# A decoder trunk on one core: the order of the first loads and of the first work on ScalarE, and the number of idle transposes

## The chip, the cores and the metric

The kernel runs on one core of a Trainium2 chip. The metric is the device time of one execution in microseconds (us); less is better. The engines are named as the profile names them: PE (TensorE, with PEld for its weight loads), DVE (VectorE), ACT (ScalarE), POOL (GpSimd) and SP (SyncE, which here issues nearly all DMAs of the opening; SPq is its queue).

## The reference

Two layers of a decoder on 256 tokens of width 2048, all in float32. Cut to what matters here:

```python
def rms_norm(x, g):
    y = x * lax.rsqrt(jnp.mean(x * x, axis=-1, keepdims=True) + EPS)
    return y * g

def hybrid_layer(x, attn_norm, w_in, ..., w_o, mlp_norm, w_up, w_down):
    h = rms_norm(x, attn_norm)
    proj = h @ w_in                      # 2048 -> 6160 columns, split in eight parts
    ...                                  # gated linear attention and stick-breaking attention
    x = x + mixed @ w_o
    hm = rms_norm(x, mlp_norm)
    return x + jnp.square(jax.nn.relu(hm @ w_up)) @ w_down

def reference(x, ...):                   # x: (1, 256, 2048)
    for l in range(2):
        x = hybrid_layer(x, ...)
    return x
```

## The kernel before

**The products.** Every float32 operand is split in a high part, rounded to the type that PE takes in one pass, and a low part, the rest. A product of a weight block with x is then three matmuls into the same accumulator: x high with weight high (L577), x high with weight low (L578), x low with weight high (L579). ACT makes high parts, DVE makes low parts. For the weights this is done in `weight_parts`: L558 is the high part (`whi`), L560 the low part (`wlo`), L547 the load of a tile of four blocks of 128 rows (`raw`).

**x as the operand.** x lies with tokens on the partitions and must be turned. `operand_parts` gives the steps for 256 of the 2048 columns: `turn` makes four transposes of 128x128 on PE (L469) into a PSUM tile, `high` takes two activations on ACT, which scale by the norm vector and round (L479), and `low` two instructions on DVE (L485). The scale is a column per 128 features, which `turn_gains` makes: one transpose of the norm vectors' rows (L316) and a copy (L317, tile `gcol_a`). The reciprocal root mean square is applied later, to the results. `norm_operand` takes the steps for two halves, a quarter of x (512 columns), one after the other.

**The opening.** The first unit, 512 columns of `w_in`, goes through 16 blocks of rows in four groups. Its first weight tile is taken block by block (`fine`), so that the first block can be used before the fourth is in. x is loaded in four quarters; the first comes in two loads (`load_x(0, parts=2)`), and quarters 1 to 3 are loaded and turned between the products, from hooks: quarter 1 after the first two blocks, which are 12 matmuls. The instructions of each engine stand in the order in which the program gives them, but for what `tc.issue_after(dep)` says: an instruction made under it comes behind `dep`. `order` gives that `dep` for each high part of the weight, from `his`, the list of x's high parts in the order in which they were made. The DMAs of the opening all stand in SP's queue.

**Idle transposes.** `wait_on_x(n)` turns the identity n times into a PSUM tile that nobody reads. `WARM0` of them stand ahead of the first work on x, `WARM1` between the turning of x's first quarter and the first product.

**Behind the opening.** The remaining projections and both attention parts follow in the order of the program. The rest of each layer (last gate columns, output projection, MLP, in the first layer also two units of the next layer's projection) is laid out by a planner, which fixes the order on each engine from assumed costs and due times.

Of the kernel before, what the change touches and what calls it, by code (L numbers as in the profile page):

```python
# [16 lines left out]

P = 128
EPS = 1e-6
WARM0, WARM1 = 8, 6  # L20
T2 = 5
STEPS = [0, 0, 1, 1, 1, 2, 3, 1, 3, 2, 3, 3, 4, 4, 5, 5, 6, 5, 5, 6, 6, 6, 7, 7]
LOADS = [0, 1, 2, 3, 4, 5, 6, 7]
# [121 lines left out]
def trunk_kernel(  # L145
# [37 lines left out]
    def open_scope(space, **want):  # L183
        if space in scopes:
            scopes.pop(space).close()
        es = scopes[space] = ExitStack()
        for key, bufs in want.items():
            pools[key] = es.enter_context(
                tc.tile_pool(
                    name=nm(key), bufs=bufs, reuse_waits="tile",  # L190
                    **({"space": PSUM} if space == "psum" else {}),
                )
            )
# [6 lines left out]
    def ps_tile():  # L200
        return pools["ps"].tile([P, 512], F32, tag="ps", name=nm("ps"))
# [8 lines left out]
    def tmp(tag, shape, dt=F32, bufs=2):  # L210
        pool = pools["att"] if tag in ATT else pools["mlp"] if tag in MLP else tpool
        return pool.tile(list(shape), dt, tag=tag, name=nm(tag), bufs=bufs)

    def att_psum():
        open_scope("psum", acc=2, ps=4)
# [20 lines left out]
    def f32(ap):  # L236
        return ap.bitcast(F32)
# [65 lines left out]
    def load_gains(b, srcs):  # L303
        r = 0
        graw[b] = tmp("t2", [P, 512], bufs=T2)[: (NA, NB)[b], :P]
        for key, src, n in srcs:
            nc.sync.dma_start(
                graw[b][r : r + DEPTH * n, :], src.rearrange("l (k p) -> (l k) p", p=P)
            )
            cols[key] = (b, r, n)  # L310
            r += DEPTH * n

    def turn_gains(b):
        n = (NA, NB)[b]
        pg = ps_tile()
        nc.tensor.transpose(pg[:, :n], graw[b], ident[:n, :n])  # L316
        return nc.vector.tensor_copy(gcol[b], pg[:, :n]).ins  # L317

    def gain(key, l, k=0):
        b, r0, n = cols[key]  # L320
        c = r0 + l * n + k
        return gcol[b][:, c : c + 1]

    def load_gate_up(l):
        kc["wg"] = tmp("wg", [RANK + 1, 512], bufs=1)
        nc.sync.dma_start(kc["wg"][0:RANK], w_gate_up[l])
        nc.sync.dma_start(kc["wg"][RANK : RANK + 1], b_gate[l : l + 1, :])
# [23 lines left out]
    def load_x(n, parts=1):  # L351
        w = 512 // parts
        for i in range(parts):
            c = n * 512 + i * w
            nc.sync.dma_start(xb[n][:, :, i * w : (i + 1) * w], xv[:, :, c : c + w])
# [6 lines left out]
    def after(n, fn):  # L362
        held.append((clock[0] + n, fn))
# [55 lines left out]
    def fast(i):  # L419
        return i in FAST  # L420

    def forms(op, i, t, tag):

        keep = tag is None

        e = []
        todo = []

        def sums():
            a11, a21, a12, a22 = (t[:, k, r * P : (r + 1) * P] for k in range(2) for r in range(2))
            n = 4 if keep else 3
            e.append(tmp("t2", [P, 512], bufs=T2)[:, : n * P].rearrange("p (k c) -> p k c", c=P))
            s = e[0][:, 3, :] if keep else a21
            nc.vector.tensor_tensor(e[0][:, 2, :], a21, a11, ALU.subtract)
            nc.vector.tensor_tensor(s, a21, a22, ALU.subtract)
            nc.vector.tensor_tensor(e[0][:, 0, :], a11, s, ALU.subtract)
            nc.vector.tensor_tensor(e[0][:, 1, :], a12, e[0][:, 0, :], ALU.subtract)

        def high():
            if e:
                if keep:
                    op.x[i] = act_tile(F32R, (P, 4, 2, P))
                else:
                    op.x[i] = tmp(tag, [P, 3, 2, P], F32R, bufs=len(FAST))
                todo.append((op.x[i], e[0]))
            todo.append((op.pair(i), t))
            for d, src in todo:
                nc.scalar.activation(d[:, :, 0, :], src, AF.Copy)  # L450

        def low():
            for d, src in todo:
                nc.vector.tensor_tensor(d[:, :, 1, :], src, f32(d[:, :, 0, :]), ALU.subtract)  # L454

        return sums, high, low

    def operand_parts(op, n, h2, key, l, place):


        i = 2 * n + h2
        got = []

        def turn():
            pt = place()
            for j in range(2):
                for tt in range(NT):
                    c = (2 * h2 + j) * P
                    nc.tensor.transpose(  # L469
                        pt[:, j * T + tt * P : j * T + (tt + 1) * P],  # L470
                        xb[n][:, tt, c : c + P], ident,
                    )
            got.extend((pt[:, j * T : (j + 1) * T], gain(key, l, 2 * i + j)) for j in range(2))

        def high():
            d = op.pair(i)
            for j, (src, g) in enumerate(got):
                his.append(
                    nc.scalar.activation(d[:, j, 0, :], src, AF.Copy, scale=g).ins  # L479
                )  # L480

        def low():
            d = op.t[i]
            for j, (src, g) in enumerate(got):
                nc.vector.scalar_tensor_tensor(  # L485
                    d[:, j, 1, :], src, g, f32(d[:, j, 0, :]), ALU.mult, ALU.subtract
                )

        def scaled():
            t = tmp("t2", [P, 2, T], bufs=T2)  # L490
            for j, (src, g) in enumerate(got):
                nc.scalar.activation(t[:, j, :], src, AF.Copy, scale=g)
            return t

        return turn, high, low, scaled

    def norm_operand(op, n, key, l, sums=False):
        for h2 in range(2):
            turn, high, low, scaled = operand_parts(op, n, h2, key, l, ps_tile)
            turn()  # L500
            if sums and fast(2 * n + h2):
                for part in forms(op, 2 * n + h2, scaled(), "sxh"):
                    part()
            else:
                high()
                low()

    def norm_squares(n, ssq):
        for tt in range(NT):
            junk = tmp("t2", [P, 512], bufs=T2)  # L510
            nc.scalar.activation(
                junk, xb[n][:, tt, :], AF.Square, accum_out=ssq[:, tt, n : n + 1]
            )

    def norm_finish(ssq):
        tot = stat(NT)
        nc.vector.tensor_reduce(tot, ssq, AX.X, ALU.add)
        return inv_rms(tot, NT, D)
# [4 lines left out]
    def wait_on_x(n):  # L523

        pw = ps_tile()
        for _ in range(n):
            nc.tensor.transpose(pw[:, :P], ident, ident)
# [259 lines left out]
    def values(acc, v):  # L787
        for tt in range(NT):
            nc.scalar.activation(
                v[:, tt, :], acc[:, tt, :], AF.Copy, scale=st["rst"][:, tt : tt + 1]  # L790
            )
        return v


    hT = Operand()
    ssq = new_ssq()
    st = {}
    his = []
    load_gains(0, (("attn", attn_norm, KT),))
    load_x(0, parts=2)  # L800
    wait_on_x(WARM0)
    st["first"] = turn_gains(0)
    norm_operand(hT, 0, "attn", 0)
    wait_on_x(WARM1)

    for l in range(DEPTH):
# [4 lines left out]
        if l == 0:  # L811
            hooks = {}

            def next_x(n):
                load_x(n)
                with tc.issue_after(st["mm"]):
                    norm_operand(hT, n, "attn", 0)

            for n, at in ((1, (0, 0)), (2, (0, 1)), (3, (1, 1))):
                hooks[at] = lambda n=n: next_x(n)  # L820

            def begin():
                st["rst"] = norm_finish(ssq)

            for n in range(4):
                after(6 + n, lambda n=n: norm_squares(n, ssq))
            after(10, begin)
            after(2, build_constants)
            after(7, load_small)
            after(11, finish_small)  # L830
            uv = unit(
                hT, wl, 0, C_SV, 512, hooks=hooks, fine=1,
                order=lambda i, k: his[4 * i + (3 if i else k)] if i or k else None,
            )
            v = tmp("v4", [P, NT, 512], bufs=2)
            after(3, lambda a=uv, b=v: values(a, b))
        else:
            open_scope("sbuf", att=1)
            att_psum()
            load_gate_up(l)  # L840
            after(2, build_constants)
            v = natural["iv"][0]
# [768 lines left out]
        hT_now, hT = hT, Operand()  # L1611
# [3 lines left out]
        for u, (kind, q, n2) in enumerate(units):  # L1615
            order, quick = unit_order(u)
# [96 lines left out]
```

## Time and profile before

| | us |
|---|---|
| median of 3 runs | 2146.02 (2145.95 to 2146.85) |
| the profiled execution | 2147.3 |
| its span, first to last instruction | 2145.6 |
| PE busy | 2134.1 (99%) |
| DVE busy | 1892.2 (88%) |
| ACT busy | 1474.0 (69%) |
| POOL busy | 159.9 (7%) |
| first product starts (from the span's start) | 8.63 |
| transposes of x's quarter 1 start | 13.34 |

Times in the trace count from the span's start. A row of the timeline gives start, duration, engine, line, operation, the tile written and the tiles read, shapes, and how many alike instructions are merged (x4); in brackets stands how long the engine had been idle before it and what ended that. The ends of matmuls are modelled, and matmuls overlap, so their pace is read from the distance of their starts. A row of the waits names who waited, for whom, the sum, the number of times and the longest.

### The profile page before, as it was taken

What the parts mean: (1) busy time and instruction counts of PE and PEld (TensorE: products, weight loads), DVE (VectorE), ACT (ScalarE), POOL (GpSimd) and SP (SyncE); (2) the same over time, 40 slices, a digit from 0 to 9 for tenths busy, and PEclk for the clock granted to TensorE, in tenths of its full rate; (3) what the DMA queues carried; (4) which work ended last, traced back from release to release, by engine and by line L of the source; (5) the groups of instructions that cost most, each with busy time, mean ns of one, the idle gap of its engine ahead of it and who ended that gap; (6) DMA issues with size and microseconds to landing.
All of it is one profiled execution on the core that took longest, in us unless ns stands there. A gap on an engine that the chain in (4) does not pass through costs nothing.

```text
span 2145.6 us, 28380 instructions
## 1 busy us (share of the span) xinstructions
PE 2134.1 (99%) x10232; PEld 1780.4 (83%) x10232; DVE 1892.2 (88%) x2533; ACT 1474.0 (69%) x1889; POOL 159.9 (7%) x210
## 2 busy tenths in 40 slices
PE   9999999999999999999999999999999999999999
PEld 7988888888888888888878888888888888888887
DVE  5677669999999999999998975799999999999998
ACT  5555356687677677678776654667876776776775
POOL 0020000000000000000001200000000000000000
PEclk9999999999999999999999999999999999999999
DMA  6655455688888878878886544657888888888886
GB/s 229 190 159 165 164 192 193 197 244 262 250 252 243 266 243 247 271 236 256 238 242 172 177 157 157 202 172 229 248 249 274 236 260 246 249 249 251 255 249 182
DMA packets 169105, 480.37 MB, mean 224 GB/s; under 512 B 9370, under 2 KB 34530, under 8 KB 168964
## 3 DMA queue, kind: packets, MB, share of 16 engines
q1 hardware_dynamic: 149380, 407.24, 55.3%
q0 software_dynamic: 19584, 71.31, 17.6%
q8 instruction: 80, 1.31, 0.2%
q14 instruction: 61, 0.50, 0.1%
HBM read 405.12 MB, written 2.10 MB: 190 GB/s over the span
## 4 chain that ended last, share of the span: by engine, by line
PE 93%; DVE 4%; DMA 1%; issue 1%; ACT 1%; SPq 0%; POOL 0%; DVEq 0%; ACTq 0%
PE acc L577 4%; PE acc L579 4%; PE acc L578 4%; PE acc L624 3%; PE acc L628 1%; DMA raw<-in_w_in_dram 1%; DVE wlo L1263 1%; DVE wlo L560 0%; DVE xb L1092 0%; PE ps L742 0%; PE ps L688 0%; PE ps L1060 0%; PE ps L706 0%; DVE t L645 0%; PE ps L1053 0%
## 5 line engine op out<-in xcount | busy, mean ns | idle before, releaser
L1259 ACT ACTIVATE whi<-raw 128x1024 fp32r<-128x1024 f32 (+1 forms) x768 | 739.9, 978 | 317.7 <-issue 45.1
L1263 DVE TENSOR_TENSOR wlo<-raw,whi 128x1024 fp32r<-128x1024 f32 (+1 forms) x632 | 690.4, 1099 | 65.0 <-ACT whi L1259 52.5
L560 DVE TENSOR_TENSOR wlo<-raw,whi 128x1024 fp32r<-128x1024 f32 (+2 forms) x162 | 181.3, 1123 | 100.0 <-ACT whi L558 99.8
L558 ACT ACTIVATE whi<-raw 128x1024 fp32r<-128x1024 f32 (+2 forms) x162 | 155.9, 968 | 158.2 <-PE acc L579 110.4
L1272 POOL DMA_DIRECT2D dlo<-raw x136 | 117.5, 865 | 1587.9 <-ACT dlo L1269 864.2
L1259 ACT ACTIVATE whi<-ts 128x1024 fp32r<-128x1024 f32 x144 | 152.8, 1061 | 72.7 <-DVE ts L1092 3.7
L577 PE MATMUL acc<-whi,act 128*128 128x512 f32 (+2 forms) x512 | 191.9, 375 | 1.0 <-ACT act L479 1.0
L578 PE MATMUL acc<-wlo,act 128*128 128x512 f32 (+2 forms) x512 | 187.2, 366 | 0.6 <-DVE wlo L560 0.6
L579 PE MATMUL acc<-whi,act 128*128 128x512 f32 (+2 forms) x512 | 187.2, 366 | 0.0
L1263 DVE TENSOR_TENSOR wlo<-ts,whi 128x1024 fp32r<-128x1024 f32 x144 | 175.9, 1222 | 10.7 <-ACT whi L1259 7.7
L1092 DVE TENSOR_TENSOR ts<-raw 128x1024 f32<-128x1024 f32 x144 | 175.9, 1222 | 1.6
L1269 ACT ACTIVATE dlo<-raw 128x1024 fp32r<-128x1024 f32 x136 | 139.3, 1046 | 3.6 <-PE m__1930_9313 L1373 1.7
L577 PEld LDWEIGHTS acc<-whi,act 128*128 128x128 f32 x512 | 97.1, 190 | 19.0 <-issue 3.0
L579 PEld LDWEIGHTS acc<-whi,act 128*128 128x128 f32 x512 | 96.8, 189 | 16.0 <-DVE act L485 0.2
L578 PEld LDWEIGHTS acc<-wlo,act 128*128 128x128 f32 x512 | 96.9, 189 | 14.7 <-DVE wlo L560 0.8
L1092 DVE TENSOR_TENSOR raw<-raw 128x512 f32<-128x512 f32 x144 | 99.3, 689 | 2.3
L1092 DVE TENSOR_TENSOR raw<-ts,raw 128x512 f32<-128x512 f32 x144 | 98.9, 686 | 0.5
L624 PE MATMUL acc<-act,whi 128*128 128x512 f32 x256 | 91.8, 401 | 0.0
L628 PE MATMUL acc<-act,wlo 128*128 128x256 f32 x256 | 71.6, 280 | 0.0
L1464 ACT ACTIVATE act<-act,st 128x512 f32<-128x512 f32 x72 | 49.2, 714 | 19.2 <-DVE act L1092 19.2
L454 DVE TENSOR_TENSOR act<-t,act 128x512 fp32r<-128x512 f32 x84 | 57.3, 686 | 0.0
L624 PEld LDWEIGHTS acc<-act,whi 128*128 128x128 f32 x256 | 48.1, 188 | 10.7
(3145 smaller groups left out, 5336.4 us busy)
## 6 DMA issues: line engine op xcount, KB each, us to landing
raw<-in_w_up_dram SPq DMA_DIRECT2D x112, 1024.0 KB, 5.4
raw<-in_w_down_dram SPq DMA_DIRECT2D x112, 1024.0 KB, 5.8
raw<-in_w_in_dram SPq DMA_DIRECT2D x82, 1024.0 KB, 5.1
dlo<-raw POOLq DMA_DIRECT2D x136, 512.0 KB, 6.5
raw<-in_w_o_dram SPq DMA_DIRECT2D x32, 1024.0 KB, 5.0
raw<-in_w_up_dram SPq DMA_DIRECT2D x32, 512.0 KB, 6.4
raw<-in_w_down_dram SPq DMA_DIRECT2D x32, 512.0 KB, 6.1
raw<-in_w_in_dram SPq DMA_DIRECT2D x18, 512.0 KB, 5.8
```

The source lines that it names most:

```text
L558: newest["hi"] = nc.scalar.activation(h, r, AF.Copy).ins
L560: newest["lo"] = nc.vector.tensor_tensor(lo[:, q : q + step, :width], r, f32(h), ALU.subtract).ins
L577: nc.tensor.matmul(o, xh[:, sl], whi[:, j, :width], start=first, stop=False)
L578: nc.tensor.matmul(o, xh[:, sl], wlo[:, j, :width], start=False, stop=False)
L579: st["mm"] = nc.tensor.matmul(o, xl[:, sl], whi[:, j, :width], start=False, stop=last).ins
L624: nc.tensor.matmul(acc[:, f, :], whi[:, j, sl], op.both(k), start=(k == 0), stop=False, skip_group_check=True,)
L628: nc.tensor.matmul(acc[:, f, T:], wlo[:, j, sl], xh, start=False, stop=(k == KT - 1), skip_group_check=True,)
L1092: nc.vector.tensor_tensor(dst, a, b, op)
L1259: nc.scalar.activation(box["h"][:, :n], src(), AF.Copy)
L1263: nc.vector.tensor_tensor(box["l"][:, :n], src(), f32(box["h"][:, :n]), ALU.subtract)
L1269: nc.scalar.activation(box["l"], src(), AF.Copy, scale=-1.0)
L1272: nc.gpsimd.dma_start(f32(box["l"]), src(), accum_op=ALU.add)
```

## The change

x's first quarter is loaded ahead of the norm vectors. Its eight transposes come ahead of that of the norm vectors on PE. `order` puts the high part of the first weight block behind x's second high part (before, it had nothing to wait for in the order), and since x's four high parts are now made ahead of it, it stands behind all four on ACT; the low parts on DVE follow in the same order. Thirteen idle transposes instead of six stand ahead of the first product.

```diff
-WARM0, WARM1 = 8, 6
+WARM0, WARM1 = 8, 13
...
     his = []
+    load_x(0, parts=2)
     load_gains(0, (("attn", attn_norm, KT),))
-    load_x(0, parts=2)
     wait_on_x(WARM0)
+    first = [operand_parts(hT, 0, h2, "attn", 0, ps_tile) for h2 in range(2)]
+    for turn, _, _, _ in first:
+        turn()
     st["first"] = turn_gains(0)
-    norm_operand(hT, 0, "attn", 0)
+    for _, high, low, _ in first:
+        high()
+        low()
     wait_on_x(WARM1)
...
             uv = unit(
                 hT, wl, 0, C_SV, 512, hooks=hooks, fine=1,
-                order=lambda i, k: his[4 * i + (3 if i else k)] if i or k else None,
+                order=lambda i, k: his[4 * i + (3 if i else max(1, k))],
             )
```

In the order of the engines, ACT begins `L479 x4, L558` where it began `L558, L479 x4`; DVE begins `L317, L485 x4, L560` where it began `L317, L560, L485 x4`; PE begins `L527 x8, L469 x8, L316, L527 x13` where it began `L527 x8, L316, L469 x8, L527 x6`; SP begins `L355 x2, L307, L547 x4` where it began `L307, L355 x2, L547 x4`. Further on in SP's queue the load of the gate's weights (L326) stands ahead of the two halves of the fourth weight tile instead of behind them.

## The prediction

> **What bounds the kernel now.** I read the page first, then TensorE's waits over the whole span, and then the timeline of the first 22 us, since the edit touches nothing else. The page's first lines and its chain:
>
> ```profile
> span 2145.6 us, 28380 instructions
> ...
> PE 2134.1 (99%) x10232; PEld 1780.4 (83%) x10232; DVE 1892.2 (88%) x2533; ACT 1474.0 (69%) x1889; POOL 159.9 (7%) x210
> ...
> PE 93%; DVE 4%; DMA 1%; issue 1%; ACT 1%; SPq 0%; POOL 0%; DVEq 0%; ACTq 0%
> ```
>
> PE is busy for 2134.1 of 2145.6 us, and the chain that ended last runs over PE for 93% of the span. So a microsecond that PE gains or loses at the start is gained or lost at the end, unless a wait later on swallows it. The waits of PE over the whole span say how few there are:
>
> ```profile
> PE ps L527 <- POOL ident masks.py:199: 1.6, 1, 1.6
> PE ps L688 <- DVE act L651: 1.3, 3, 0.9
> PE acc L577 <- ACT act L479: 1.0, 1, 1.0
> ...
> PE ps L469 <- DMA xb<-in_x_dram: 0.6, 1, 0.6
> ```
>
> The three in the opening are 1.6 us for the identity that GpSimd builds, 1.0 us for x's high part on ScalarE, and 0.6 us for x itself. The longest group behind the opening sums to 1.3 us, so hardly anything later can swallow a gain. The order of the instructions, built for both versions and laid beside each other engine by engine, differs in the opening alone, apart from one wait that changes places between two products of the later stage and one small load (below): everything behind about 20 us stands as before. What the change is worth is therefore what it does to the moment at which PE is through with the first products.
>
> The opening, from the timeline (start, duration, engine, line):
>
> ```profile
> 0.82 0.40 SPq L307 DMA_DIRECT2D t<-in_attn_norm_dram  x1
> ...
> 1.28 0.93 SPq L355 DMA_DIRECT2D xb<-in_x_dram  x2
> ...
> 2.25 1.89 SPq L547 DMA_DIRECT2D raw<-in_w_in_dram  x4
> ...
> 3.45 0.31 PE L316 MATMUL ps<-ident,t 32*128 32x32 f32 x1
> ...
> 3.80 0.19 DVE L317 COPY gcol_a<-ps 128x32 f32<-128x32 f32 x1 [3.80 <-PE ps L316]
> ...
> 4.34 1.97 PE L469 MATMUL ps<-ident,xb 128*128 128x128 f32 x8 [0.58 <-DMA xb<-in_x_dram]
> ...
> 6.10 1.49 PE L527 MATMUL ps<-ident 128*128 128x128 f32 x6
> ```
>
> PE turns the identity eight times while it waits (L527), turns the norm vectors (L316), then x's first quarter (L469, eight transposes), then the identity six times more. x was waited for until 4.34. What ends the wait for the first product:
>
> ```profile
> 7.59 0.63 ACT L558 ACTIVATE whi<-raw 128x512 fp32r<-128x512 f32 x1 [5.48 <-DMA raw<-in_w_in_dram]
> 8.12 1.55 ACT L479 ACTIVATE act<-ps,gcol_a 128x256 fp32r<-128x256 f32 x4
> 8.25 0.69 DVE L560 TENSOR_TENSOR wlo<-raw,whi 128x512 fp32r<-128x512 f32 x1 [4.26 <-ACT whi L558]
> ...
> 8.63 0.79 PE L577 MATMUL acc<-whi,act 128*128 128x512 f32 x1 [1.04 <-ACT act L479]
> ...
> 8.98 1.66 DVE L485 SCALAR_TENSOR_TENSOR act<-ps,gcol_a,act 128x256 fp32r<-128x256 f32 x4
> ...
> 9.22 0.63 PE L578 MATMUL acc<-wlo,act 128*128 128x512 f32 x1
> ...
> 9.55 1.68 ACT L558 ACTIVATE whi<-raw 128x512 fp32r<-128x512 f32 x3
> 9.65 0.66 PE L579 MATMUL acc<-whi,act 128*128 128x512 f32 x1
> ...
> 10.55 1.89 DVE L560 TENSOR_TENSOR wlo<-raw,whi 128x512 fp32r<-128x512 f32 x3
> ```
>
> The weight's first block lands, ScalarE rounds it (L558) at 7.59, and only then makes x's four high parts (8.12, one every 1.43/4 = 0.36 us, since the next L558 starts at 9.55). The first product starts at 8.63, when x's first high part is there. The second (L578) starts at 9.22, 0.28 us after the weight's low part is ready (8.25 + 0.69 = 8.94). The products from there:
>
> ```profile
> 12.24 0.57 PE L579 MATMUL acc<-whi,act 128*128 128x512 f32 x1
> ...
> 12.65 0.39 PE L577 MATMUL acc<-whi,act 128*128 128x512 f32 x1
> ...
> 13.34 1.03 PE L469 MATMUL ps<-ident,xb 128*128 128x128 f32 x8
> ...
> 14.13 0.47 PE L577 MATMUL acc<-whi,act 128*128 128x512 f32 x1
> ```
>
> Here lies the money. The second product starts at 9.22 and the ninth at 12.24: 0.43 us each. From 12.65 they come every 0.23 us. The same holds for transposes: eight took 1.76 us at 4.34 (to 6.10, 0.22 each) and 0.79 us at 13.34 (to 14.13, 0.10 each). PE thus ran at half pace from its start until somewhere between 12.24 and 12.65, and at full pace afterwards. The windows view prints a granted clock of 1.00 even for the first 10 us, so the slow part is seen only in the spacing of the rows. PE had by then worked without a longer gap for 3.6 to 4.0 us, counted from 8.63; before that stands a stop from about 7.4 (six transposes of 0.22 from 6.10) to 8.63.
>
> **The change, part by part.**
>
> *x ahead of the norm vectors.* The two loads of x take the queue slots at 0.82 and 1.28 instead of those at
>
> ```profile
> 1.28 0.41 SPq L355
> ...
> 1.75 0.46 SPq L355
> ...
> 2.25 5.32 DMA raw<-in_w_in_dram
> ```
>
> so they are issued 0.46 us earlier, the norm vectors take the slot at 1.75, and the four loads of the weight keep theirs (2.25 on). I let x land 0.46 earlier too, since the first load's time runs from its issue and nothing is ahead of it. Then the eight transposes start at 4.34 - 0.46 = 3.88 and end at 5.64. The second half of x, issued at 1.75 before, was there by 5.22 (half of the eight transposes passed without a stop), so 16 KB of norm vectors in that slot, behind the same bytes, are there by 5.64 too. Their transpose and copy took 3.99 - 3.45 = 0.54 us: the gains are ready at 6.18, where before they were ready at 3.99 and hidden.
>
> *x's high parts ahead of the weight's.* ScalarE was idle until 7.59; now the four high parts run at 6.22 and take 1.43 us, to 7.65. The weight landed at 2.25 + 5.32 = 7.57, so its high part starts at 7.65 instead of 7.59, ends at 8.28, and the low part on VectorE runs from 8.31 to 9.00. x's low parts (L485) stand ahead of it in VectorE's queue: four took 1.66 us, so 0.39 apart, the first behind x's first high part at 6.7, the last started by 7.9, so the queue is free at 8.3. The second product then starts at 9.28 against 9.22: **+0.06 us**. So the reordering alone buys nothing: the first product no longer waits for ScalarE, but the second waits for VectorE as before. If x lands no earlier than before, the gains come at 6.64 and everything here is +0.52; if x and the weight both came earlier, the high parts still hold the weight's until 7.65. The term lies in 0.06 to 0.52, and I take 0.06 since the row of the first load is the direct one.
>
> *Thirteen transposes instead of six.* They start by 5.95 (5.64 + 0.31 of L316) and at 0.22 each end at 8.81. The first product, whose operands are ready at 8.33, starts there and has its 0.43 us by 9.24, ahead of the second's 9.28: the fillers cost nothing, but only 0.04 us is to spare, and each one more at half pace would cost 0.2. What they do is close the stop of 7.4 to 8.63: from 3.88 on PE has no gap worth the name. If transposes count as work for whatever sets the pace, full pace comes 4.0 us after 3.88, at 7.9, 1.4 us ahead of the second product. The 8 intervals from the second product to the tenth then take 8 x 0.23 = 1.84 instead of 12.65 - 9.22 = 3.43: **-1.59 us**. If fillers get faster in the middle, PE idles up to 0.7 us ahead of the second product; a stop of such length did not slow it elsewhere, as the transpose behind a wait of 0.92 us shows, at 0.30 us against 0.43 of a slow one (1.97 - 7 x 0.22):
>
> ```profile
> 1209.96 0.30 PE L688 MATMUL ps<-ident,act 128*128 128x128 f32 x1 [0.92 <-DVE act L651]
> ```
>
> The Trainium skill, "TensorE: Matmul & The Clock Gate", Part 1, puts the change of pace at the end of a busy stretch of about 3.4 us whose boundaries run freely. By it full pace here would come anywhere from 7.3 to 10.7, and the term would be about -0.9 to -1.6 (an estimate from that page); the 3.6 to 4.0 us above agree with it, and no run here shows the scatter yet.
>
> *Can the next things keep up at full pace?* The weight's four blocks are issued 0.47 apart (1.89/4) and took
>
> ```profile
> raw<-in_w_in_dram SPq DMA_DIRECT2D x4, 256.0 KB, 5.4
> ```
>
> so the second is in at 2.72 + 5.4 = 8.1 and the fourth at 9.1; before, the fourth's L558 was started by 10.6 without a wait. The second's high part is ready at 8.8 and its low part, 0.60 behind the first's (three L560 took 1.89), at 9.6; its products are due at 9.28 + 5 x 0.23 = 10.4. The third and fourth are ready by 11.3 at the worst and due behind the next transposes, at 12.6. Those turn x's second quarter. It and the third are issued at
>
> ```profile
> 4.18 0.43 SPq L355 DMA_DIRECT2D xb<-in_x_dram  x1
> ...
> 6.13 0.68 SPq L355 DMA_DIRECT2D xb<-in_x_dram  x1
> ```
>
> and the five loads of x took from issue to landing
>
> ```profile
> DMA to landing us min/median/max: 3.2/6.7/8.8
> ```
>
> so the second quarter is in at 10.9 by the median, against a start of 13.34 - 1.53 = 11.8, and the third at 14.9 by the longest, against
>
> ```profile
> 16.99 1.03 PE L469 MATMUL ps<-ident,xb 128*128 128x128 f32 x8
> ```
>
> 16.99 - 1.53 = 15.5: 0.6 us of slack, the narrowest spot, since the DMA engines are full here:
>
> ```profile
> 10.00:12.00 2.00, 2.00 (x6) 1.52 (x6) 2.00 (x5) 1.23 (x3) 0.00 (x0) 1.00 1.02 388
> ```
>
> One small load, the gate's weights (L326), moves in SyncE's queue ahead of two of the weight's:
>
> ```profile
> 12.47 0.88 SPq L547 DMA_DIRECT2D raw<-in_w_in_dram  x2
> ...
> 13.39 0.46 SPq L326 DMA_DIRECT2D wg<-in_w_gate_up_dram  x1
> ```
>
> SyncE stood still there until VectorE had freed a buffer, up to 12.47, so the 0.46 us slot is hidden; uncovered, it would put the weight's fourth tile back by that. So nothing takes the gain back.
>
> **Sum.** -1.59 + 0.06 = -1.53 us, against the profiled execution's 2147.3 (span 2145.6 and 1.7 around it): 2145.8. The median of the runs is 2146.02, 1.28 below that execution; the difference carried over gives **2144.5 us**, 0.07% less. About 0.2% (4.3 us) is what a measurement of this kernel can tell from no change, so the likeliest outcome is one within it.
>
> **The rivals.**
>
> *Transposes do not count.* Then the pace changes some 4.0 us after the first product, at 12.7 or so, as before, and what is left is +0.06: 2146.1. For it: 22 transposes between 1.55 and 7.4 did not bring full pace. Against it: that stretch has stops (3.76 to 4.34 and 7.4 to 8.63), and transposes do follow the pace. The Trainium skill, same page, Part 4, states this rival as a rule: in transpose mode the full clock "doesn't engage", since it does not count as PE-busy the same way. By that rule the time would be 2146.1; the trace of before can neither bear it out nor refute it.
>
> *Slower: the norm vectors become the late operand.* All four high parts now need the gains, and the weight's high part stands behind them. From the point where x (and with it the gains) lands less than 0.52 us earlier than before, each tenth delays the second product by a tenth, up to +0.52; with the pace unchanged as well, that gives 2146.02 + 0.52 = 2146.5, and should the later start of the gapless stretch cost one more slow product, 2146.7. For it: the gains have no cover any more (ready at 6.18, needed at 6.12). Against: nothing stands ahead of x in the queue.
>
> *The change of pace comes, but x's later quarters land late.* If the third quarter is 0.6 us later than the longest row allows, the gain shrinks by as much, to -0.9: 2145.1.
>
> **How the numbers follow.** Full pace early, 0.60 (the late quarter's case, 0.07, in it); transposes not counted, 0.26; gains late, 0.10; something I do not see, 0.04. The predicted time is the first one's, 2144.5. Downwards the range takes one execution's distance from the median, 1.28: 2143.2. Upwards it holds both no-gain cases and the distance of the highest run from the median (0.83): 2146.9. None of these cases reaches 4.3 us: what is unseen is split into faster 0.04 and slower 0.03, and within 0.2% stands 0.93.
>
> **What would show it.** In the changed profile: the first L469 at 3.9 and not 4.34; L316 at about 5.65 with L317's copy over by 6.2; four L479 ahead of the first L558, and that one at 7.6 to 7.7; PE without a gap from 3.9 to the first product near 8.4 to 8.8; the second product near 9.3; products every 0.23 us from there, and the transposes of x's second quarter at 11.8. Products still 0.43 apart until past 12 would refute the main step and confirm the first rival; an L558 at 8.1 would confirm the second. A start of the transposes of the third quarter with a DMA wait ahead of it would show the last.

## The result, and the profile after

| | before | after |
|---|---|---|
| median of 21 runs each, us | 2146.75 (2145.41 to 2147.95) | 2150.38 (2147.70 to 2153.49) |
| ratio | | 1.0015, interval 1.0009 to 1.0022 |
| profiled execution, us | 2147.3 | 2149.33 |
| runs with a mean granted clock below 1 | 3 of 35, 1 of 33, 6 of 27, 2 of 15 (four later sets) | 17 of 21 |

The changed kernel is slower, by some 3.6 us at the medians, which is within the 0.2% that the prediction called no change but outside its range. The first page of after:

```profile
span 2147.6 us, 28393 instructions
...
PE 2134.8 (99%) x10239; PEld 1780.0 (83%) x10239; DVE 1893.3 (88%) x2533; ACT 1473.0 (69%) x1889; POOL 159.1 (7%) x210
...
q8 instruction: 80, 1.31, 0.2%
```

Seven matmuls more, as the edit says, and nearly the same busy times. The last line is a DMA queue that the prediction left out: 80 pieces of 16 KB. The opening, from the timeline of after (start, duration, engine, line):

```profile
0.82 0.94 SPq L355 DMA_DIRECT2D xb<-in_x_dram  x2
1.82 0.46 SPq L307 DMA_DIRECT2D t<-in_attn_norm_dram  x1
...
3.89 1.89 PE L469 MATMUL ps<-ident,xb 128*128 128x128 f32 x8 [0.38 <-DMA xb<-in_x_dram]
...
5.72 0.25 PE L316 MATMUL ps<-ident,t 32*128 32x32 f32 x1
...
5.89 1.64 PE L527 MATMUL ps<-ident 128*128 128x128 f32 x13
6.00 0.19 DVE L317 COPY gcol_a<-ps 128x32 f32<-128x32 f32 x1 [6.00 <-PE ps L316]
6.23 1.57 ACT L479 ACTIVATE act<-ps,gcol_a 128x256 fp32r<-128x256 f32 x4 [4.13 <-DVE gcol_a L317]
...
7.10 1.66 DVE L485 SCALAR_TENSOR_TENSOR act<-ps,gcol_a,act 128x256 fp32r<-128x256 f32 x4 [0.91 <-ACT act L479]
...
7.67 2.44 ACT L558 ACTIVATE whi<-raw 128x512 fp32r<-128x512 f32 x4
...
8.37 0.49 PE L577 MATMUL acc<-whi,act 128*128 128x512 f32 x1 [0.83 <-ACT whi L558]
8.68 2.49 DVE L560 TENSOR_TENSOR wlo<-raw,whi 128x512 fp32r<-128x512 f32 x4
...
9.41 0.50 PE L578 MATMUL acc<-wlo,act 128*128 128x512 f32 x1 [0.55 <-DVE wlo L560]
...
9.75 0.40 PE L579 MATMUL acc<-whi,act 128*128 128x512 f32 x1
...
11.83 0.39 PE L579 MATMUL acc<-whi,act 128*128 128x512 f32 x1
...
12.06 1.03 PE L469 MATMUL ps<-ident,xb 128*128 128x128 f32 x8
```

The opening did what was forecast: x turned at 3.89, the norm vectors at 5.72, the high parts at 6.23, the weight's at 7.67. The thirteen idle transposes take 1.64 us, so they already run at full pace, and from the third product on they follow every 0.23 us. One thing differs from the forecast: at full pace the idle transposes are over by 7.5 us, and PE stands still for 0.83 us ahead of the first product and 0.55 us ahead of the second. The second quarter of x is turned at 12.06, 1.28 us ahead of before's 13.34. That lead is gone by the end. Laid beside each other matmul by matmul, after leads by about 1.3 us up to 1090, by 0.92 at 1211, by nothing at 1361.6, and is 1.93 behind at 1367.5 and 2.05 at the end. The waits of PE over the whole span of after show the place:

```profile
PE ps L688 <- DVE act L651: 1.4, 3, 1.0
...
PE m__2553_12344 L1377 <- ACT whi L1264: 0.8, 1, 0.8
PE m__2553_12344 L1378 <- DVE wlo L1268: 0.8, 1, 0.8
```

The last two stand at the second layer's planned stage (lines behind the edit are 5 higher in after than in before). The windows view of after there (stretch; length, then busy time and instructions of PE, PEld, DVE, ACT, POOL; granted clock; DMA share; GB/s), and PE's timeline:

```profile
1360.67:1364.08 3.41, 1.89 (x8) 1.23 (x7) 2.25 (x2) 3.41 (x5) 0.00 (x0) 1.00 0.08 31
1364.08:1367.50 3.42, 3.42 (x10) 2.64 (x9) 2.25 (x4) 3.36 (x6) 0.00 (x0) 0.50 0.61 163
1367.50:1370.91 3.41, 3.41 (x16) 2.81 (x15) 2.52 (x3) 3.35 (x6) 0.00 (x0) 1.00 0.69 213
```

```profile
1361.56 0.50 PE L1377 MATMUL m__2553_12344<-whi,act 128*128 128x512 f32 x1 [0.76 <-ACT whi L1264]
1362.82 0.50 PE L1378 MATMUL m__2553_12344<-wlo,act 128*128 128x512 f32 x1 [0.76 <-DVE wlo L1268]
...
1364.08 0.61 PE L1377 MATMUL m__2554_12345<-whi,act 128*128 128x512 f32 x1
1364.49 0.63 PE L1378 MATMUL m__2554_12345<-wlo,act 128*128 128x512 f32 x1
```

PE waits twice for 0.76 us, is busy for 1.89 of 3.41 us, and then runs for 3.41 us at a granted clock of 0.50: 10 matmuls where the next window has 16. The half-pace stretch costs 1.6 us (the loss grows from 0.35 to 1.93 across it). Before had one wait there, in PE's timeline:

```profile
1362.47 0.50 PE L1373 MATMUL m__2553_12337<-wlo,act 128*128 128x512 f32 x1 [0.53 <-DVE wlo L1263]
```

What PE waits for is the high part of the stage's first weight tile, and that for the tile's load. ScalarE's row in before's timeline, and in after's:

```profile
1360.09 1.06 ACT L1259 ACTIVATE whi<-raw 128x1024 fp32r<-128x1024 f32 x1 [1.22 <-DMA raw<-in_w_in_dram]
```

```profile
1360.45 1.06 ACT L1264 ACTIVATE whi<-raw 128x1024 fp32r<-128x1024 f32 x1 [2.50 <-DMA raw<-in_w_in_dram]
```

The load was issued at 1351.76 in before and at 1350.83 in after: 8.33 us from issue to use, and 9.62. What else moved in the meantime shows in the DMA view, for 1357.5 to 1359.5 in after (queue, kind: packets, MB, share):

```profile
q1 hardware_dynamic: 393, 0.78, 101.7%
q8 instruction: 1, 0.02, 3.0%
```

and for the same stretch in before:

```profile
q1 hardware_dynamic: 384, 0.76, 100.8%
```

One 16 KB piece of kind "instruction", which takes 0.95 us, runs inside the load in after, while the DMA engines are full with it. In before it comes at 1360.05, when the tile is in. The pieces come once for about 256 instructions of PE: 10239 matmuls and as many weight loads over 80 pieces. That they are PE's is inferred from this count. Seven more transposes are 14 more instructions, so every later piece is due 14 instructions earlier in the program.

### The profile page after: what moved, and what is told of

Its sections match the earlier page's. It is cut to its first block, busy times and chain, and to the rows that moved or that the text cites. A ratio compares the mean times of both kernels' runs of the same rounds, so it can differ in the third digit from the quotient of the medians.

```text
span 2147.6 us, 28393 instructions
## 1 busy us (share of the span) xinstructions
PE 2134.8 (99%) x10239; PEld 1780.0 (83%) x10239; DVE 1893.3 (88%) x2533; ACT 1473.0 (69%) x1889; POOL 159.1 (7%) x210
## 4 chain that ended last, share of the span: by engine, by line
PE 93%; DVE 4%; DMA 1%; issue 1%; ACT 1%; POOL 0%; SPq 0%; DVEq 0%; ACTq 0%
PE acc L577 4%; PE acc L578 4%; PE acc L579 4%; PE acc L624 3%; PE acc L628 1%; DVE wlo L1268 1%; DMA raw<-in_w_in_dram 1%; DVE wlo L560 0%; DVE xb L1097 0%; PE ps L742 0%; PE ps L688 0%; PE ps L1065 0%; PE ps L706 0%; DVE t L645 0%; PE ps L1058 0%
## 5 line engine op out<-in xcount | busy, mean ns | idle before, releaser
L560 DVE TENSOR_TENSOR wlo<-raw,whi 128x1024 fp32r<-128x1024 f32 (+2 forms) x162 | 180.9, 1121 | 94.9 <-ACT whi L558 94.7
L558 ACT ACTIVATE whi<-raw 128x1024 fp32r<-128x1024 f32 (+2 forms) x162 | 155.8, 967 | 153.0 <-PE acc L579 110.8
L579 PEld LDWEIGHTS acc<-whi,act 128*128 128x128 f32 x512 | 96.4, 188 | 15.6
```

The costliest lines, as they stand in the source:

```text
L558: newest["hi"] = nc.scalar.activation(h, r, AF.Copy).ins
L560: newest["lo"] = nc.vector.tensor_tensor(lo[:, q : q + step, :width], r, f32(h), ALU.subtract).ins
L579: st["mm"] = nc.tensor.matmul(o, xl[:, sl], whi[:, j, :width], start=False, stop=last).ins
```

## The experiments

The theories, with the letters that the expectations use: **A**, the half pace comes from the holes of the opening, or of the second layer, by their place against the clock's windows. **B**, the lead is lost wherever PE comes too early for a load. **C**, the longer list of PE moves a piece of the instruction stream into the load of the planned stage's first tile, and that holds the tile up. **D**, the lead itself makes PE wait there. C and D were formed on the traces of the first four runs.

**The changed kernel again.** No edit.

> The changed kernel once more, for a second trace. Two theories of why it takes 2150.4 though its profiled opening was 1.3 us ahead. A (half pace again): idle transposes bring full pace by about 5.6, but at full pace thirteen of them are over by 7.4, and PE then stands still for about 1.0 us ahead of the first product and 0.8 us ahead of the second; where such holes, or those of the second layer near 1361, make up half of a stretch of 3.41 us, PE drops to half pace for the next 3.41 us, 1.6 us each. Expected: 2150 to 2151, and a trace with at least one half-pace stretch, its place different from 1364 if the stretches are cut at another place. B (the lead is lost at waits): the opening is ahead by 1.3 in every run and weight loads that land late swallow it and more; expected: waits on loads grow by 3 us or more against before, no half-pace stretch needed.

Measured: 2151.04 (2145.86 to 2154.05), ratio 1.0016 (1.0007 to 1.0024). The loss repeats. Its trace has the full opening lead (1.08 us), the same two waits at 1361 (ScalarE waits 2.55 us for the tile), and no half pace, which A expected in it. Eight of 12 runs have a granted clock below 1.

**The transposes alone, on before's order.**

```diff
-WARM0, WARM1 = 8, 6
+WARM0, WARM1 = 8, 13
```

> The kernel before with thirteen idle transposes instead of six, nothing else. A: the norm vectors' transpose and x's stay where they were, the stretch from 4.34 is nearly without a gap, so full pace comes at about 9 or earlier; if it comes early, the fillers end early and the hole ahead of 8.63 is back; time between -1.5 and +3.5 against before, with a share of runs showing a granted clock of 0.999. B: the first product cannot start before 8.63, so the opening gains up to 1.5 and the later waits take it: 0 to +3.5 with the clock at 1.000.

Measured: 2150.21, ratio 1.0014 (1.0006 to 1.0023). So the transposes bring the whole loss, without any change of order. Matmul by matmul against before, its trace gains 1.25 us in the opening and loses 1.3 at 297, where the first layer has the same stage, 0.9 and then a half-pace stretch (1.6) at 1209, and 1.1 at 1361.

**The order alone, on six transposes.**

```diff
-WARM0, WARM1 = 8, 13
+WARM0, WARM1 = 8, 6
```

> The changed kernel with six idle transposes instead of thirteen: the loads and ACT's order alone. A: the hole from about 7 to 8.4 is longer still; if full pace comes early (window with eight transposes of x) it is lost again, otherwise it comes where it did before, at 12 to 13: 2146.8 to 2150, and clock 0.999 in the runs above 2149. B: the opening is as before to within 0.2 us and so is the end: 2146.5 to 2147.5.

Measured: 2148.46, ratio 1.0005 (0.9996 to 1.0014). In its trace nothing is lost at 297 or 1361. Its own cost stands in the opening. PE's timeline:

```profile
5.85 0.87 PE L527 MATMUL ps<-ident 128*128 128x128 f32 x6
8.32 0.50 PE L577 MATMUL acc<-whi,act 128*128 128x512 f32 x1 [1.60 <-ACT whi L558]
9.36 0.80 PE L578 MATMUL acc<-wlo,act 128*128 128x512 f32 x1 [0.54 <-DVE wlo L560]
9.95 0.63 PE L579 MATMUL acc<-whi,act 128*128 128x512 f32 x1
10.38 0.63 PE L577 MATMUL acc<-whi,act 128*128 128x512 f32 x1
...
14.22 1.70 PE L469 MATMUL ps<-ident,xb 128*128 128x128 f32 x8
```

PE had full pace by 5.3 us (six transposes in 0.87 us), lost it over the hole of 1.60 us, and kept half pace to 15.6. So the fillers do have a use with this order.

**A full hole: 22 transposes.**

```diff
-WARM0, WARM1 = 8, 13
+WARM0, WARM1 = 8, 22
```

> The changed kernel with twenty-two idle transposes, which at full pace (0.109 us each) end at about 8.3, when the first product's operands are ready. A: the hole ahead of the first product is closed, one of 0.8 us ahead of the second is left: no half pace in the opening, the time 2145.5 to 2147 in runs where full pace comes by 6; where it comes later, the fillers hold the first product up, by 2.4 us at most. B: the time stays at about 2150, since the opening's lead is the same and is lost later.

Measured: 2149.34, ratio 1.0011 (1.0003 to 1.002). The opening hole ahead of the first product is closed and full pace comes at 5.0; the traced execution is the lowest of its 11 runs (2146.51). The median is 2.7 us above before's 2146.62 all the same, so A's first half gets no support.

**The longer list with before's opening.** Seven idle transposes at about 22 us, behind all of the opening.

```diff
+LATE = 7
...
+            if (n, h2, key, l) == (3, 0, "attn", 0):
+                for _ in range(LATE):
+                    nc.tensor.transpose(pt[:, :P], ident, ident)
```

> The kernel before with its opening untouched and seven idle transposes at about 22 us, at full pace, ahead of those of x's last quarter: no lead, but PE's list is as much longer as in the changed kernel. Theory C: PE's instructions come in pieces of 16 KB (the page's instruction queue q8: 80 packets, 1.31 MB), one for every 256 instructions of PE; fourteen more instructions (seven transposes with their weight loads) move the piece that is fetched near 1360 us from just behind the landing of the second layer's first weight tile of its planned stage into it, which lands 1.2 us later, and PE's longer wait there brings half pace for 3.41 us more often. Expected: 0.8 for the transposes, 1.2 for the landing, 1.6 in about three runs of four: 2149 to 2150.5, clock 0.999 in half of the runs or more, and a first weight landing of 9.4 to 9.7 us behind its issue instead of 8.3. Rival D: what counts is that PE comes early to that wait by the opening's lead. Here it comes late by 0.8: 2147.4, clock 1.000.

Measured: 2149.88, ratio 1.0021 (1.0012 to 1.003), on a chip where before had 2145.9. There is no lead here, and the seven cost at most 0.8 us themselves (0.11 each at full pace). The loss is there, so D falls, and B with it. But the place that C named is not where this trace lost: the tile was used 8.48 and 8.45 us after its issue in the two layers, not 9.4 to 9.7, and there was no half pace. ScalarE's row in its timeline:

```profile
1360.90 1.06 ACT L1263 ACTIVATE whi<-raw 128x1024 fp32r<-128x1024 f32 x1 [1.34 <-DMA raw<-in_w_in_dram]
```

The traced execution (2148.07) lies 1.8 us below the median of its runs. Behind the seven transposes (0.8) it lost 0.7 us at 1209, where PE waits 1.64 us for VectorE, and 0.1 to 0.2 at 297 and 1361. So this run shows that the longer list costs time, and not where. With sixteen:

> The same with sixteen late transposes (32 more instructions of PE). C: the piece is fetched some 3 us ahead of its place before, early enough that the tile's landing is hardly held up (8.3 to 8.7): 1.75 for the transposes and little else, 2148.0 to 2149, clock 0.999 in a third of the runs at most; that is, hardly slower or even faster than with seven. D: 2146.6 + 1.75 = 2148.4, clock 1.000; the two theories differ on the pair with seven, not on this one alone.

Measured: 2150.08, ratio 1.0022 (1.0014 to 1.0031). I had expected the piece to come early enough to harm little. It came at 7.15 us after the issue, not earlier, and the tile was held up (ScalarE waits 2.30 us at 1361 and 2.33 at 297). The count of instructions moves the piece, but not by a fixed time.

**The whole change, with the list as long as before's.** Seven transposes fewer ahead of x, where PE waits for x anyway.

```diff
-WARM0, WARM1 = 8, 13
+WARM0, WARM1 = 1, 13
```

> The changed kernel with one idle transpose instead of eight ahead of x and thirteen behind it: PE's list is as long as before, the lead of the opening stays. C: the piece near 1360 is fetched where it was before, the landing is 8.3 to 8.5 again, the lead is kept: 2145.3 to 2146.3, clock 0.999 in one run of five at most. D: the lead makes PE wait longer there all the same: 2149 to 2151 and clock 0.999 in half of the runs or more.

Measured: 2146.7, ratio 1.0006 (0.9997 to 1.0014), one run of 11 with a granted clock below 1. That is 0.8 us above before's median of 2145.9, a little more than C allowed, so the lead of the opening doesn't show in the time. The lead in its trace's opening is 0.81 us, and ScalarE's wait at 1361 is before's again, though the piece did not come where it was before: 7.73 us after the issue, against 8.29.

```profile
1359.59 1.06 ACT L1264 ACTIVATE whi<-raw 128x1024 fp32r<-128x1024 f32 x1 [1.25 <-DMA raw<-in_w_in_dram]
```

**The same with seven more behind x**, so that the list is as long as the changed kernel's.

```diff
-WARM0, WARM1 = 8, 13
+WARM0, WARM1 = 1, 20
```

> The changed kernel with one idle transpose ahead of x and twenty behind it: PE's list is as long as the changed kernel's, and the hole that thirteen leave ahead of the first product at full pace is closed. C: the piece is fetched as in the changed kernel, so the landing is 9.4 to 9.7, and the time 2149.5 to 2151 with clock 0.999 in most runs. A (the holes of the opening make the half pace): 2145.5 to 2147, clock 1.000.

Measured: 2151.15, ratio 1.0023 (1.0014 to 1.0032), 6 of 11 below 1. The two kernels differ in seven idle transposes, and their openings end nearly alike (leads of 0.81 and 1.13 us at the second quarter of x); their medians are 4.5 us apart. The windows view at 297 of this trace:

```profile
295.21:298.63 3.42, 1.64 (x7) 0.81 (x6) 1.35 (x2) 2.73 (x4) 0.00 (x0) 1.00 0.19 73
298.63:302.04 3.41, 3.41 (x10) 2.67 (x9) 2.49 (x3) 3.35 (x6) 0.00 (x0) 0.50 0.33 56
```

So A's first half falls for good, since the opening's hole is filled here. Over the ten traces up to this one the tile of either layer was used 9.4 to 9.9 us after its issue in 8 cases. In each of these a piece of the instruction stream began 7.1 to 7.8 us after the issue. In 6 other cases the piece began then too, and the tile was used after 8.4 to 8.5. Where the piece began at other times (6 cases: 6.2, 6.8, or 8.3 and later), the tile was used after 8.2 to 8.7. A late tile was thus seen only with a piece inside that stretch, and in about half of those cases. With the longer list the piece fell into the stretch in 12 of 14 cases, with before's in 2 of 6.

What decides between the two halves shows in the single DMA packets of these ten traces. Each 1 MB load is closed by sixteen packets of 4 bytes, as many as there are DMA engines, and the tile is used 0.4 to 1.2 us after the last of them. In the 12 cases that weren't late the last one follows the fifteenth within 0.18 us. In each of the 8 late ones fifteen are in and the last lags by 0.6 to 1.3 us. While a piece runs, about 15 packets of 2 KB start every 0.08 us where 16 did, so the piece takes up one engine. In the six cases with a piece and no late tile it is the next tile whose last closing packet lags (by 0.35 to 1.17 us). So the tile is late when the engine that takes the piece still has a share of the tile to bring. When the piece began, 8 to 13 of the sixteen had closed theirs.

**Taking the tile out of reach.** SyncE issued a 1 MB load for the output projection ahead of the stage's first two weight tiles. It now stands behind them. This makes the tile early whatever holds it up, so it tests the place and not the pieces.

```diff
+        first = {}
...
+                if x == 4:
+                    with tc.issue_after(first[0]), tc.issue_after(first[2]):
+                        nc.sync.dma_start(dst, src)
+                elif x < 4:
+                    first[x] = nc.sync.dma_start(dst, src).ins
-                if by_columns(u, i):
+                elif by_columns(u, i):
```

On the kernel before:

> The kernel before, with one edit behind the opening: in each layer's planned stage the 1 MB load for the output projection that SyncE issues ahead of the stage's first two weight tiles is issued behind them. Theory C (a 16 KB piece of the instruction stream, fetched into the transfer of that weight tile, holds it up by some 1.3 us; how far it does depends on the number of PE instructions ahead): the tile that is landing 8.3 us after its issue lands after 5 to 7 us, the waits of PE at 297 (0.6 us in the kernel before's trace) and 1361 (0.5) vanish, and the time is 0.5 to 2 us below before's. Theories A and D (holes of the opening; the lead itself): the waits at 297 and 1361 vanish as well if the load is earlier, about -1 us, no more. If the load is not earlier (something else holds it up), the waits stay.

Measured: 2144.89 (2143.72 to 2146.27), ratio 0.9988 (0.9979 to 0.9997). The tile's load is issued 3.7 us earlier than in before's trace, and its last closing packet comes 5.0 us after the issue instead of 7.9. SyncE's rows in the timelines of before and of this run:

```profile
1351.76 0.97 SPq L1232 DMA_DIRECT2D raw<-in_w_in_dram  x2
```

```profile
1348.04 0.92 SPq L1230 DMA_DIRECT2D raw<-in_w_in_dram  x2
```

ScalarE's row at that place has no wait for a DMA any more, and PE waits for nothing at 297 or 1361:

```profile
1356.98 1.04 ACT L1265 ACTIVATE whi<-raw 128x1024 fp32r<-128x1024 f32 x1
```

On the changed kernel:

> The changed kernel with the same edit of the planned stage. Theory C: with the tile in early no piece of the instruction stream can make PE wait there, so the changed kernel's loss behind the opening is gone: time 1.5 to 3 us below before's, and at or below the run with the edit of the stage alone; granted clock 1.000 in nearly all runs; no PE wait over 0.3 us at 297 and 1361. Theory D (the lead makes PE wait elsewhere) or A: still 3 to 4 us above the run with the edit of the stage alone, with the loss at other places of the trace.

Measured: 2146.07 (2145.32 to 2148.24), ratio 0.9995 (0.9987 to 1.0004). The edit is worth 1.0015 - 0.9995 = 0.20%, 4.3 us, on the changed kernel and 0.12%, 2.6 us, on before. So about half of the 0.15% by which the change is slower goes away with this place (0.08%, 1.7 us). The other half stays: the changed kernel is still 0.07% (1.5 us) above the kernel before with the same edit, though the intervals overlap. That lies between what C and what D and A gave; C's 1.5 to 3 us below before were not reached (1.1 by the medians). Its trace shows one more place, the wait for L651 on VectorE at 1209, and the windows around it:

```profile
PE ps L688 <- DVE act L651: 1.9, 3, 1.4
```

```profile
1207.45:1210.86 3.41, 1.75 (x12) 1.28 (x11) 3.41 (x5) 2.35 (x3) 0.00 (x0) 1.00 0.08 26
1210.86:1214.27 3.41, 3.41 (x11) 2.73 (x10) 3.41 (x6) 2.12 (x5) 1.05 (x1) 0.50 0.48 135
```

At 1209 PE waits twice in a row for it: 1.45 and 0.21 us here, 0.18 and 0.21 in the kernel before with the edit, 0.92 and 0.21 in before itself. Over the fourteen traces the first of the two waits is 1.45 to 1.86 us in four of the nine with a longer list, and 1.00 or less in the other five and in all five with before's length. The same edit with one transpose ahead of x (WARM0, WARM1 = 1, 13):

> The changed kernel with the same edit of the planned stage and with one idle transpose instead of eight ahead of x (the list of PE is then as long as before's). Theory C: the length of the list no longer matters, so within 0.5 us of the run with all transposes, plus what the later full pace costs (0.5 us): 1 to 2.5 us below before's. If the length of the list still matters at some other place, it is 1 us or more below the run with all transposes.

Measured: 2145.6 (2144.64 to 2148.48), ratio 0.9990 (0.9982 to 0.9999). And before with the edit and the seven late transposes:

> The kernel before with the edit of the planned stage and with seven idle transposes at 22 us: the opening is before's, the list of PE is as long as the changed kernel's. The same seven cost 3.3 to 4 us without the edit of the stage. Theory C, with the held-up tile as the only place: no more than their own 0.8 us above the run with the edit of the stage alone (2144.9), so 2144.9 to 2145.7. If the length of the list also matters at another place, about 1.2 us or more above it, 2146 and over, as the changed kernel with the same edit (2146.1); what that kernel lost would then not be due to its lead.

Measured: 2146.94 (2145.89 to 2149.1), on a chip where before had 2147.94; ratio 0.9998 (0.9989 to 1.0007). Without the edit the seven stood 0.21% above before, with it 0.10% above before with the edit, of which their own 0.8 us are 0.04%. What is left, 0.06%, is no more than the intervals allow. By the medians it is 1.2 us above the run with the edit of the stage alone, each against before on its own chip, which is the second case of the expectation and not the first. In this trace it stands at 1209 (the first wait for VectorE is 0.99 us, against 0.18), nothing is lost at 297 or 1361.

| kernel | PE's list | opening | ratio to before |
|---|---|---|---|
| changed | longer | changed | 1.0015 |
| before, 13 transposes | longer | pace only | 1.0014 |
| before, 7 late | longer | before's | 1.0021 |
| before, 16 late | longer | before's | 1.0022 |
| changed, 1 and 20 | longer | changed | 1.0023 |
| changed, 22 | longer | changed | 1.0011 |
| changed, 6 | as before | order only | 1.0005 |
| changed, 1 and 13 | as before | changed | 1.0006 |
| before, tile early | as before | before's | 0.9988 |
| changed, 1 and 13, tile early | as before | changed | 0.9990 |
| changed, tile early | longer | changed | 0.9995 |
| before, 7 late, tile early | longer | before's | 0.9998 |

Pair by pair the longer list costs time whatever the opening is: 0.14% (before and 13), 0.21 and 0.22% (before and 7 or 16 late), 0.17% (1 and 13 against 1 and 20), 0.09% (1 and 13 against the changed one). Against the changed kernel with six, whose opening cost it 1.5 us in its trace, thirteen cost 0.10% and twenty-two 0.06%. Once the tile is early, the longer list costs 0.05 to 0.1% (1 and 13 against the changed one; before and 7 late). An interval of one ratio is some 0.09% to either side, so the small differences say something only together; the late seven and the pair of 1 and 13 and 1 and 20 stand clear alone. So C holds for the length of the list as the cause, and for the tile as the place of about half of the loss in the changed kernel. Seven more transposes behind both planned stages, which would leave the pieces ahead of them where they are, were not tried. What the remaining 0.05 to 0.1% is, or whether it is there at all, stays open: single traces put it at 1209, and the intervals are as wide as it is. The edit of the planned stage alone beats both kernels; the opening added nothing to it that these runs can tell.

One more loss belongs to the changed order and not to the list. Between 1090 and 1120, where VectorE is busy for 29.8 of the 30 us in before and in after, all eight traces with the changed order lose 0.24 to 0.30 us against before's trace, and the five others with before's order lose nothing there (0.01 at most). What in the order does it was not tried.

## Why the prediction was wrong, by its own steps

**"Nothing takes the gain back", "everything behind about 20 us stands as before".** This is the step that failed. The order of the instructions did stand as before, and I took that for their timing. I went through what the lead would meet in the first 17 us, and did not ask what a longer list does to the fetching of that list. In its place the runs showed this: a longer list alone, with before's opening, costs 0.21% (seven late transposes), and in the changed kernel about half of the loss goes away with the late tile. The wait of 1.2 us that ScalarE had for the tile at 1361 in before was in the trace, and PE's 0.53 behind it; there was no slack at all at that place, and the sum had no term for it. The failed term by the traces of after and before: 2.05 + 1.28 = 3.3 us, of which 1.3 are the longer waits at 1361 (from 0.92 ahead to 0.35 behind), 1.6 the half pace behind them, and 0.4 to 0.5 smaller steps between, 0.3 of them at 1090 to 1120, where all traces with the changed order lose as much.

**The size of the gain, -1.59 us.** The mechanism was right and the baseline was not. The untouched opening reached full pace at 12.62 us in the execution that I was given, and at 7.64, 10.05, 10.77 and 7.34 in the traces of the four other kernels that have it (the runs with late transposes and those with the early tile on before). PE's timeline of the first of these, whose opening is before's:

```profile
9.52 0.50 PE L583 MATMUL acc<-whi,act 128*128 128x512 f32 x1
9.85 0.40 PE L581 MATMUL acc<-whi,act 128*128 128x512 f32 x1
10.09 0.39 PE L582 MATMUL acc<-wlo,act 128*128 128x512 f32 x1
```

Its products are 0.23 apart from the third on. Half the time from 9.22 to the change of pace is lost, so the five executions lose 1.7, 0, 0.4, 0.8 and 0: 0.6 on average. That is what closing the hole is worth, not 1.59. The start of the transposes of x's second quarter says the same of the whole opening: 13.34, 12.54, 11.76, 12.80 and 11.95 in these five, 12.48 on average, and 12.06, 12.26 and 12.17 in the three traces with the whole change, 12.16 on average. The opening gained 0.3 us and not 1.53. I carried 1.28 us from the execution to the median on top, although that distance was probably in part the same late change of pace, counted twice; it rested on three runs, and by the median of 21 (2146.75) it is 0.55.

**The second product at 9.28.** It came at 9.41. The low parts of x started at 7.10, behind the second high part and not the first at 6.7, so VectorE's queue was free at 8.68 instead of 8.3. The term is +0.19 instead of +0.06. That VectorE and not ScalarE bounds it was right, and so were the loads: x 0.45 us earlier, no wait for x's second or third quarter.

**Transposes count (first rival, 0.26).** They do. The identity's and x's transposes alone, with no product yet, brought full pace ahead of the first product in after (5.6 us) and in seven other traces (5.0 to 8.5). The Trainium skill, "TensorE: Matmul & The Clock Gate", Part 4, says that the full clock doesn't engage in transpose mode; in these traces it did for float32 transposes, which the trace prints as MATMUL without naming a mode. Part 1 of that page, free-running windows of 3.4 us, is borne out: between the first full pace and the end of the work all half-pace stretches are 3.41 us long or twice that, and they stand on a grid whose place differs from trace to trace.

**The slower rivals.** Neither of them happened; the slower outcome had its mechanism 1300 us further on, and it was in none of my cases. I had put 0.04 on something unseen and given it no place in the range, whose upper end held the cases without a gain and one run's distance from the median (0.83).

## What to carry to other kernels

A kernel that keeps PE busy for 99% of 2 ms can still have places without slack far behind an edit: read the waits there (a load that ends just ahead of its use, here 1.2 us late for ScalarE) before writing that nothing can take a gain back. Adding instructions to an engine, idle ones too, moved the later pieces of its instruction stream here; try such an edit also with the number of instructions kept the same. Size a term that hangs on a free-running window from several executions, not from one.

## What was not expected of the hardware

- The instruction stream comes through the same DMA engines as the data, in pieces of 16 KB, one for about 256 instructions of PE, 0.9 to 1.5 us each. A piece near the end of a 1 MB load put the use of the load back by 0.9 to 1.5 us in 8 of 14 cases, when the engine that took the piece still had a share of the load to bring.
- Half pace needs no stop of 3.4 us. Over all fourteen traces, behind the opening, every grid window in which PE was busy for more than 1.9 of 3.41 us was followed by full pace; of the six with 1.9 or less, five were followed by half pace (busy 1.39, 1.53, 1.64, 1.75, 1.89) and one was not (1.68). The Trainium skill, "TensorE: Matmul & The Clock Gate", the table of advice in "Why this matters for your kernels", allows gaps up to about 3 us; here two waits of 0.76 us that fell into one window were enough.
- VectorE slows beside GpSimd here. Its L560, 1.22 us elsewhere, took 1.98 in the changed kernel with the early tile while GpSimd worked:

```profile
1201.05 1.98 DVE L560 TENSOR_TENSOR wlo<-raw,whi 128x1024 fp32r<-128x1024 f32 x1
```

```profile
1201.92 3.52 POOL L945 TENSOR_TENSOR act<-act,row 128x512 f32<-128x512 f32 x2
```

It took 2.00 in before and in before with the early tile as well, where PE's waits behind it were 1.1 and 0.4 us against 1.7 here, so this alone does not set the wait at 1209.
